# Moving ten DRAM sums of FFN weight blocks to other items of a two-layer encoder kernel

## The chip, the cores and the metric

The kernel runs on one core of a Trainium2 chip. The metric is device time in microseconds: the median of the runs shown. Lower is better. The engines are named as in the profile: PE is TensorE (matmuls), PEld its weight loads, DVE is VectorE, ACT is ScalarE, POOL is GpSimd, SP is SyncE, which here only issues DMAs.

## The reference

Two layers, sequence 512, model width 1024, all in float32. Each layer mixes tokens in three branches of the same input, gates and sums them, projects, normalises, and ends with a SwiGLU feed-forward network:

```python
for l in range(DEPTH):
    h = x @ w_in[l]
    rq, rk, rv, rg, cq, ck, cv, dq, dk, dv, gates = split(h)
    o_a = retention(rq, rk, rv, rg)
    o_b = chunk_attention(cq, ck, cv, ca_rel_bias[l])
    o_c = diff_attention(dq, dk, dv, lam)
    g = sigmoid(gates + b_merge[l])
    merged = g[0]*(o_a @ w_branch_a[l]) + g[1]*(o_b @ w_branch_b[l]) + g[2]*(o_c @ w_branch_c[l])
    x = layer_norm(ALPHA*x + merged @ w_out[l])
    u_gate, u_up = split(x @ w_ffn_in[l])
    x = layer_norm(ALPHA*x + (silu(u_gate)*u_up) @ w_ffn_out[l])
```

The FFN's hidden width is 2816. Retention has 4 heads, the chunk attention 8, the differential attention 4.

## The kernel before, in words

**Arithmetic.** Every float32 operand of a matmul is carried as a pair of rounded parts, high and low; `mm3` (L131 to L134) makes a product of three matmuls. A weight block is loaded into a staging tile `st`; ACT casts it into the high part `wh` (L164 or L385), DVE subtracts to get the low part `wl` (L165 or L392). There are four staging tiles (`NSTAGE`) and three pairs of `wh` and `wl` (`AHEAD`), so loads and casts run up to three blocks ahead of PE.

**Sums of weight blocks.** The large projections use a product of 2x2 blocks with seven block products in place of eight. For that, some products need sums of two or more blocks of the same weight matrix. The sums are made by DMA: POOL issues a DMA whose data is added to what its destination holds (`accum_op=ALU.add`, "an accumulate" below). Mostly that goes into a staging tile (`more`, L191). For the fifth column block of `w_ffn_in` (class `KnownEarly`, two sums) and two row groups of `w_ffn_out` (class `KnownAll`, four sums each) the sums are made long before, in DRAM, by `Known.step` (L325 to L336). Each of these ten steps a layer has two parts: `begin` makes a DRAM tile and has SP copy a first block of 1 MB into it (L331), ordered after the DMA that SP was given last; `end` has POOL add a second block (L335), which waits until the copy has landed. The FFN later loads the finished sums as plain blocks.

The steps in order are in0a, in0c, out00y, out00x, out00c, out00h, out01y, out01x, out01c, out01h (the first digit is the layer, so in1a and so on in the second). out00x adds out00y to its own copy, out00h adds out00x; out01x and out01h likewise.

**The order of the work.** A layer's token mixer is a hand-written list of items in `layer`. An item is a set of weight blocks, a function that issues its matmuls, and groups of smaller steps that `between` calls after each half of it. `run_items` issues them in that order, loads ahead; the framework's scheduler then places each instruction in its engine's queue, so an instruction with few dependencies can stand earlier in a queue than its step stands in the list. Each engine runs its queue in order.

In the list, counted from 0 with the layer's opening items, 18 to 29 are the end of retention (heads 2 and 3, first projections of the second branch, gate of the third), 30, 31, 33 and 35 are the first branch's output (`u_branch(0, i)`) beside the heads of the chunk attention, 36 to 47 the second branch's output and the differential attention, 48 to 54 the third branch, 55 on the output projection `w_out` (`out_items`, whose class `Late` also accumulates on POOL).

In `u_branch` the gate's tile `th` of the first branch comes back from DRAM: SP loads it (L1297), and DVE multiplies it with the branch's product in PSUM, `pt` (L1299). Around it DVE does the softmax of the chunk attention: `tb` is a bias table loaded by SP (L1091), the reduction at L557 reads the scores `psc` and releases their PSUM bank, ACT exponentiates (L559), DVE scales (L1108), PE transposes (`ptr`, L572), ACT and DVE split the result in `cPh` and `cPl` (L116, L122), and PE multiplies them with the values into `pco` (L1142). `memset`s of `kl` on POOL (L514, L515) clear halves of new key tiles.

POOL also computes the power `rsr` of the retention's and the differential attention's norms (L1024, L1234) from a sum `ss` of DVE; DVE scales the head with it (`do`, L1237) and PE transposes it (`pdt`, L1247).

Before the change, one step ends and the next begins at every second item from 30 on:

```python
SUMS_AT = range(30, 52, 2)
...
sums = [list(fns) for fns in zip([lambda: None, *ends], [*begins, lambda: None])]
```

so the begins stand at 30, 32, ... 48 and the ends at 32, 34, ... 50.

Of the kernel before, what the change touches and what calls it, by code (L numbers as in the profile page):

```python
# [51 lines left out]


GROUPS = [(0, 4), (8, 4)]
SUMS_AT = range(30, 52, 2)
REST = 16


# [1 line left out]
def trunk(ctx, tc, x_in, xT_in, w_in, ret_norm_g, da_norm_g, lq1, lk1, lq2, lk2, w_a, w_b, w_c, b_merge, w_out,  # L60
# [614 lines left out]
    def item(specs, fn, *groups):  # L675

        items.append((specs, fn, groups))
# [84 lines left out]
    def layer(l):  # L762
# [80 lines left out]
        def u_rqk(dst, base, hp):  # L843
            def fn(wt):
                for j in range(2):
                    rqk_done(dst, 2 * hp + j, proj_T(xT, wt, P * j))
                    between()
            return [([wcols(base + 256 * hp, 256)], KT)], fn
# [97 lines left out]
        def s_dh(h):  # L946
            def fn():
                dhs[h] = g(name="dh")
                nc.sync.dma_start(dhs[h], decay[h])
            return fn  # L950
# [3 lines left out]
        def s_kt(h):  # L954
            def fn():
                r = rkf.pop(h)
                ps = bank("pkt")
                for mt in range(2):
                    sl = slice(P * mt, P * mt + P)
                    nc.tensor.transpose(ps[:, sl], r[:, sl], ident)  # L960
                kT[h] = HalfPair("kT")
                for mt in range(2):
                    sl = slice(P * mt, P * mt + P)
                    split(kT[h], ps[:, sl], cols=sl, scale=rcol[:, 6 * h + mt:6 * h + mt + 1])
            return fn

        def s_kv(h):
            def fn():
                k, hp, hc = kT.pop(h), h // 2, slice(256 * (h % 2), 256 * (h % 2) + 256)
                ps = bank("pkv")[:, :256]  # L970
                for mt in range(2):
                    sl, vp = slice(P * mt, P * mt + P), rv[hp, mt]
                    mm3(ps, k.hi[:, sl], k.lo[:, sl], vp.hi[:, hc], vp.lo[:, hc], mt == 0, mt == 1)
                kv[h] = HalfPair("kv")
                split(kv[h], ps)
            return fn

        def s_r1(h):
            def fn():
                dh = dhs.pop(h)  # L980
                rp[h] = [Pair("rp"), HalfPair("rp")]
                q, k = rq.pop(h), rk.pop(h)
                rqb[h] = q[1]
                for b, w in enumerate((256, P)):
                    ps, tmp = bank("psr"), g(name="rtmp")
                    for i in range(2):
                        mt = b + 2 * i
                        msl, o = slice(P * mt, P * mt + P), w * i
                        mm3(ps[:, o:o + w], k.hi[:, msl], k.lo[:, msl], q[i].hi[:, P * b:], q[i].lo[:, P * b:], True, True)
                    if b == 0:  # L990
                        nc.vector.tensor_mul(tmp, ps, dh)
                    else:
                        nc.vector.tensor_mul(tmp[:, :P], ps[:, :P], dh[:, :P])
                        nc.vector.scalar_tensor_tensor(tmp[:, P:2 * P], ps[:, P:2 * P], SHIFT[h], dh[:, 2 * P:3 * P],
                                                       op0=ALU.mult, op1=ALU.mult)
                    split(rp[h][b], tmp[:, :2 * w], cols=slice(0, 2 * w))
            return fn
# [39 lines left out]
        def s_r3(h):  # L1037
            def fn():
                os_ = rps.pop(h)
                for d in range(2):  # L1040
                    ps = bank("prt")
                    for nt in range(NT):
                        nc.tensor.transpose(ps[:, P * nt:P * nt + P],
                                            os_[nt // 2][:, 256 * (nt % 2) + P * d:256 * (nt % 2) + P * d + P], ident)
                    oa[2 * h + d] = Pair("oa")
                    split(oa[2 * h + d], ps, scale=v["rg"][:, d:d + 1])
            return fn
# [16 lines left out]
        def v_back(dst):  # L1064
            def fn():
                for k, away in list(dst.items()):
                    dst[k] = g(F32R, "vhl")
                    nc.sync.dma_start(f(dst[k]), away)
            return fn
# [8 lines left out]
        def u_cqk(p):  # L1078
            def fn(wt):
                cqk[p] = QK()  # L1080
                cqk[p].set_q(proj_T(xT, wt, 0), -CA_DH ** -0.5)
                between()
                cqk[p].set_k(proj_T(xT, wt, P))
            return [([wcols(CQ + P * p, P), wcols(CK + P * p, P)], KT)], fn
# [27 lines left out]
        def s_c2(h):  # L1112
            def fn():
                cP[h] = triangle("cP")
                transpose_triangle(cE.pop(h), cP[h])
            return fn
# [155 lines left out]
        def u_gate(br, i):  # L1272
            def fn(wt):
                for j, d in enumerate(tiles(br, i)):
                    gate_done(br, d, proj_T(xT, wt, P * j), (br, i) in EARLY)
                    between()
            return [(cols_of(W, GATE + D * br, br, i), KT)], fn
# [39 lines left out]
        def s_mleft(k):  # L1317
            def fn():
                mq[k].left(acc[k], acc[k + 4], 0.5)
            return fn  # L1320
# [11 lines left out]
        def c_narrow(h):  # L1332
            return lambda: cqk[h // 2].narrow(h % 2)

        def d_narrow(h, j):
            return lambda: dqk[h].narrow(j)

        def c(i):

            return (([s_c3(i - 2, c_narrow(i))] if i >= 2 else []) + [s_c1(i)],  # L1340
                    [s_c2(i - 1)] if 0 <= i - 1 < CA_HEADS else [])

        def d(i):

            h, j = divmod(i, 2)
            if j == 0:
                mid = [s_d4(h - 2)] if h >= 2 else []
                mid += [s_d2(h - 1)] if h >= 1 else []
            else:
                mid = [s_d3(h - 1)] if h >= 1 else []  # L1350
            return mid, [s_d0(h, j)]
# [82 lines left out]
        fifth = KnownEarly(f"in{l}", w_ffn_in[l], 0, 4, (512 * 4, FFN + 512 * 4))  # L1434
        out_blocks = [KnownAll(f"out{l}{i}", w_ffn_out[l], *gr) for i, gr in enumerate(GROUPS)]
        begins, ends = zip(*(st for hv in [fifth] + out_blocks for st in hv.steps()))
        sums = [list(fns) for fns in zip([lambda: None, *ends], [*begins, lambda: None])]
        o = proj = out_items()

        def u_rvg(hp):  # L1440
# [15 lines left out]
        for at, ((specs, fn), *groups) in enumerate(start + [  # L1456
            (w["x"], [p["a"]]), (u_gate(0, 3), [s_kt(0)], [s_kt(1)]), (w["g"],), (w["h"], [p["c"]]),
            (p["m1"], [s_dh(0)]), (p["y"], [], [s_r1(0)]), (p["v"], [s_dh(1)]), (p["m2"], [], [s_r1(1)]),
            (p["x"], [q["a"]]), (u_rqk(rq, RQ, 1), [s_kv(0)], [s_kv(1)]), (p["g"], [q["c"]]), (p["h"],),
            (q["m1"], [], [s_r2(0)]), (q["y"], [s_r2(1)]), (u_rqk(rk, RK, 1), [], [s_r3(0)]),  # L1460
            (q["v"], [s_dh(2)]), (q["m2"], [s_r3(1), s_kt(2)], [s_kt(3), s_r1(2)]), (q["x"], [s_dh(3)]), (u_cqk(0), [], [s_kv(2)]), (q["g"], [s_kv(3)], [s_r1(3)]), (q["h"],),
            (u_gate(2, 0), [s_r2(2)], [s_r2(3), s_r3(2)]), (u_cqk(1), [s_r3(3)] + c(0)[0], c(0)[1]),
            (u_branch(0, 0), c(1)[0] + [v_back(cv)], c(1)[1]), (u_branch(0, 1), *c(2)), (u_cqk(2), *c(3)),
            (u_branch(0, 2), *c(4)), (u_cqk(3), *c(5)), (u_branch(0, 3), *c(6)), 
            (u_dqk(0), [s_c2(6), s_c3(5, c_narrow(7))], [s_c1(7)]), (u_gate(1, 0), [s_c3(6)], [s_c2(7)]),
            (u_dqk(1), [v_back(dv), s_c3(7, d_narrow(0, 0))] + d(0)[1]), (u_branch(1, 0), *d(1)),
            (u_gate(1, 1), [], d(2)[1]), (u_branch(1, 1), [s_d2(0)], d(3)[1]), (u_dqk(2), [s_d3(0)]),
            (u_gate(1, 2), *d(4)), (u_branch(1, 2), *d(5)), (u_dqk(3),),
            (u_gate(1, 3), *d(6)), (u_branch(1, 3), *d(7)), (u_gate(2, 1), [gates_in(2, 0), s_d4(2)], [s_d2(3)]),
            (u_gate(2, 2), [s_d3(3)], [rows_in, s_d4(3)]),  # L1470
            (u_branch(2, 0), [o["a"]], [s_mleft(0)]), (u_branch(2, 1), [], [s_mleft(1)]), (u_gate(2, 3), [s_mright(0)], [s_mright(1), o["c"]]),
            (u_branch(2, 2),), (u_branch(2, 3), [], [s_mleft(2), s_mleft(3)]),
            (o["m1"], [s_mright(2)]), (o["m2"], [s_mright(3)]), (o["y"],), (o["v"],), (o["x"], [norm_rows]),
            (o["g"], [], [s_turned(0)]), (o["h"],),
        ]):
            if at in SUMS_AT:
                groups.append(sums[SUMS_AT.index(at)])
            item(specs, fn, *groups)


        hid = [None] * FT
# [296 lines left out]
```

## Time and profile before

| | |
|---|---|
| median of 3 runs | 1859.38 us (1859.22 to 1859.66) |
| the profiled execution | 1861.9 us, its span 1860.1 us |
| granted clock of TensorE | 0.999 |
| DMA | 344.85 MB, mean 185 GB/s |
| POOL waiting for the copy of in0a, at 287.59 us | 30.43 us |
| POOL waiting for the copy of out01y, at 395.04 us | 16.19 us |

Times are microseconds from the span's start. In a timeline a row is: start, duration, engine, line, operation, output<-inputs, shape, and in brackets the idle time of the engine before it with what ended it. "SPq" is SP's queue. A row of the DMAs gives the tile and its source, the queue that issued it, the count, the size and the median time from issue to landing. A list of waits names who waited for whom, with the total, the number of times and the longest.

### The profile page before, as it was taken

The page shows a single profiled execution, that of the slowest core. Times are in us where ns is not written, and L with a number is a line of the kernel's source. Part 1 is how long each engine was busy: PE and PEld are TensorE (multiplying, and loading weights), DVE is VectorE, ACT ScalarE, POOL GpSimd, SP SyncE. Part 2 cuts the span into 40 slices and gives each one's busy share as a digit, 9 for nine tenths or more (in the row PEclk, how much of TensorE's full clock was granted, in tenths as well). Part 3 has the DMA queues.
Part 4 walks back from the last instruction along what each step waited for, and adds up shares of the span by engine and source line. Part 5 has one row for each costly group of instructions (what it writes and reads, how often), then busy time and mean ns, then how long its engine had stood idle before and what let it go on. Part 6 is the DMA issues. An engine that isn't in the chain of part 4 may idle for free. (4 is left out here: it accounts for less than half of the span.)

```text
span 1860.1 us, 23455 instructions
## 1 busy us (share of the span) xinstructions
PE 1845.1 (99%) x8772; PEld 1539.5 (83%) x8772; DVE 1380.5 (74%) x2102; ACT 1019.6 (55%) x1645; POOL 140.6 (8%) x156
## 2 busy tenths in 40 slices
PE   9999999999999999999999999999999999999998
PEld 7888888788887888888888888888888878888887
DVE  6766755777669786689696777566776797866997
ACT  5555554576645645565465556555766465455551
POOL 2001000011001000000020010001010010000000
PEclk9999999999999999999999999999999999999999
DMA  9685447796475866774586844568955677767652
GB/s 291 177 270 151 124 142 221 186 248 166 133 206 149 197 221 159 184 235 147 182 244 186 245 120 143 169 175 216 254 142 153 176 179 183 210 171 186 225 175 75
DMA packets 244706, 344.85 MB, mean 185 GB/s; under 512 B 9316, under 2 KB 111824, under 8 KB 244592
## 3 DMA queue, kind: packets, MB, share of 16 engines
q1 hardware_dynamic: 213024, 281.84, 45.7%
q0 software_dynamic: 31424, 61.26, 19.1%
q8 instruction: 69, 1.13, 0.2%
q14 instruction: 45, 0.37, 0.1%
q10 hardware_dynamic: 144, 0.26, 0.0%
HBM read 321.25 MB, written 64.01 MB: 207 GB/s over the span
## 5 line engine op out<-in xcount | busy, mean ns | idle before, releaser
L392 DVE TENSOR_TENSOR wl<-st,wh 128x2048 fp32r<-128x2048 f32 (+1 forms) x159 | 353.0, 2222 | 138.2 <-ACT wh L385 131.2
L385 ACT CAST wh<-st 128x2048 fp32r<-128x2048 f32 x154 | 294.1, 1913 | 218.8 <-PE pf L134 110.6
L132 PE MATMUL pt<-xTh,wh 128*128 128x512 f32 x832 | 327.6, 394 | 0.5 <-DVE mx L557 0.5
L133 PE MATMUL pt<-xTl,wh 128*128 128x512 f32 x832 | 324.3, 390 | 0.2 <-DVE xTl L740 0.2
L134 PE MATMUL pt<-xTh,wl 128*128 128x512 f32 x832 | 324.4, 390 | 0.0
L165 DVE TENSOR_TENSOR wl<-st,wh 128x1024 fp32r<-128x1024 f32 (+2 forms) x170 | 177.8, 1064 | 58.6 <-ACT wh L164 54.1
L164 ACT CAST wh<-st 128x1024 fp32r<-128x1024 f32 (+2 forms) x170 | 153.3, 924 | 86.5 <-PE pt L133 53.3
L134 PEld LDWEIGHTS pt<-xTh,wl 128*128 128x128 f32 x832 | 156.3, 188 | 33.2
L132 PEld LDWEIGHTS pt<-xTh,wh 128*128 128x128 f32 x832 | 156.7, 188 | 32.5 <-DVE mx L557 1.2
L133 PEld LDWEIGHTS pt<-xTl,wh 128*128 128x128 f32 x832 | 156.5, 188 | 31.5 <-DVE xTl L740 0.5
L132 PE MATMUL pf<-wh,xTh 128*128 128x512 f32 x384 | 151.0, 394 | 0.2
L134 PE MATMUL pf<-wh,xTl 128*128 128x512 f32 x384 | 149.3, 391 | 0.1
L133 PE MATMUL pf<-wl,xTh 128*128 128x512 f32 x384 | 149.2, 389 | 0.0
L132 PE MATMUL pf<-wh,s12h 128*128 128x512 f32 x288 | 113.7, 395 | 0.0
L132 PE MATMUL pf<-wh,s43h 128*128 128x512 f32 x288 | 112.9, 392 | 0.0
L133 PE MATMUL pf<-wl,s12h 128*128 128x512 f32 x288 | 112.3, 390 | 0.0
L133 PE MATMUL pf<-wl,s43h 128*128 128x512 f32 x288 | 112.2, 390 | 0.0
L134 PE MATMUL pf<-wh,s43l 128*128 128x512 f32 x288 | 111.9, 390 | 0.0
L134 PE MATMUL pf<-wh,s12l 128*128 128x512 f32 x288 | 111.7, 390 | 0.0
L911 ACT COPY tc<-pf 128x512 f32<-128x512 f32 x96 | 54.9, 587 | 76.7 <-PE pf L134 75.9
L132 PEld LDWEIGHTS pf<-wh,xTh 128*128 128x128 f32 x384 | 72.1, 188 | 17.2 <-ACT xTh L116 1.5
L134 PEld LDWEIGHTS pf<-wh,xTl 128*128 128x128 f32 x384 | 72.1, 188 | 16.1 <-DVE xTl L122 0.7
(392 smaller groups left out, 3741.1 us busy)
## 6 DMA issues: line engine op xcount, KB each, us to landing
st<-in_w_in SPq DMA_DIRECT2D x53, 1024.0 KB, 6.6
st<-in_w_ffn_in SPq DMA_DIRECT2D x46, 1024.0 KB, 5.3
st<-in_w_in SPq DMA_DIRECT2D x48, 512.0 KB, 5.2
st<-in_w_ffn_in POOLq DMA_DIRECT2D x20, 1024.0 KB, 11.0
st<-in_w_ffn_out SPq DMA_DIRECT2D x16, 1024.0 KB, 5.1
st<-in_w_in POOLq DMA_DIRECT2D x12, 1024.0 KB, 11.5
th<-th SPq DMA_DIRECT2D x40, 256.0 KB, 6.1
st<-in_w_out SPq DMA_DIRECT2D x10, 1024.0 KB, 5.1
```

The costliest lines, as they stand in the source:

```text
L132: nc.tensor.matmul(ps, lh, rh, start=start, stop=False, skip_group_check=onto)
L133: nc.tensor.matmul(ps, lh, rl, start=False, stop=False, skip_group_check=onto)
L134: nc.tensor.matmul(ps, ll, rh, start=False, stop=stop, skip_group_check=onto)
L164: return [nc.scalar.copy(self.hi[:, a:b], self.st[:, a:b]), nc.vector.tensor_sub(self.lo[:, a:b], self.st[:, a:b], f(self.hi[:, a:b]))]
L165: nc.vector.tensor_sub(self.lo[:, a:b], self.st[:, a:b], f(self.hi[:, a:b]))]
L385: nc.scalar.copy(self.hi, st)
L392: nc.vector.tensor_sub(self.lo[:, k], self.st[:, k], f(self.hi[:, k]))
L911: nc.scalar.copy(t[to, j], ps)
```

## The change

The rule "every second item" is replaced by two tables, one for the ten copies and one for the ten accumulates, and an item may have both. The steps, their order, their sizes and the blocks they read stay the same, and so does everything that reads the sums.

```diff
 GROUPS = [(0, 4), (8, 4)]
-SUMS_AT = range(30, 52, 2)
+COPIED_AT = [18, 21, 24, 27, 37, 40, 43, 45, 47, 49]
+ADDED_AT = [21, 24, 27, 29, 40, 43, 45, 47, 49, 51]
 REST = 16
...
         begins, ends = zip(*(st for hv in [fifth] + out_blocks for st in hv.steps()))
-        sums = [list(fns) for fns in zip([lambda: None, *ends], [*begins, lambda: None])]
+        sums = {}
+        for at, fn in [*zip(ADDED_AT, ends), *zip(COPIED_AT, begins)]:
+            sums.setdefault(at, []).append(fn)
...
-            if at in SUMS_AT:
-                groups.append(sums[SUMS_AT.index(at)])
-            item(specs, fn, *groups)
+            item(specs, fn, *groups, sums.get(at, []))
```

in0a, in0c, out00y and out00x are copied at 18, 21, 24 and 27 and added to at 21, 24, 27 and 29; the other six are copied from 37 to 49 and added to from 40 to 51. No step stands at 30 to 36 any more. The file has one line more than before, so every line from 56 on is one higher in the changed kernel. Instructions that are the same in both kernels can stand in another order in their engine's queue, as the scheduler places them anew; the numbers behind the names of tiles shift with them. Three places:

SP's queue in the first branch of layer 0, around the load of the fifth gate tile (th_2824, source th0_0_4), with bias tables (tb) and the next weights (st); before:

```order
L1091 DMA tb_2727<-nrel_85 128x512
L331 DMA in0c_2814<-in_w_ffn_in 128x4x512
L160 DMA st_3417<-in_w_branch_b 128x4x256
L1297 DMA th_2824<-th0_0_4_583 128x512
L1091 DMA tb_2868<-nrel_85 128x512
L1297 DMA th_2899<-th0_0_5_626 128x512
```

Now:

```order
L1092 DMA tb_2737<-nrel_85 128x512
L161 DMA st_3418<-in_w_branch_b 128x4x256
L332 DMA out00c_3517<-in_w_ffn_out 128x4x512
L1298 DMA th_2831<-th0_0_4_583 128x512
L1092 DMA tb_2875<-nrel_85 128x512
L1298 DMA th_2906<-th0_0_5_626 128x512
```

The copy of in0c ahead of the weights is gone, and the copy of out00c has come up between the weights and the gate tile.

DVE's queue at the same place: the end of one head (cot), the gate's multiply (th, with the product pt), and the softmax's reductions (cE and mx, from the scores psc) of the next head; before:

```order
L1147 TENSOR_TENSOR cot_2852<-pco_2853,cos_2865 64x512
L1299 SCALAR_TENSOR_TENSOR th_2824<-th_2824,pt_2826 128x512
L557 ISA cE_2871,mx_2875<-psc_2876,tb_2727 128x512
L557 ISA mx_2875 128x1
L557 ISA cE_2872,mx_2875<-psc_2881,tb_2727 128x384
```

Now:

```order
L1148 TENSOR_TENSOR cot_2859<-pco_2860,cos_2872 64x512
L558 ISA cE_2878,mx_2882<-psc_2883,tb_2737 128x512
L558 ISA mx_2882 128x1
L558 ISA cE_2879,mx_2882<-psc_2888,tb_2737 128x384
L558 ISA mx_2882 128x1
L558 ISA cE_2880,mx_2882<-psc_2893,tb_2737 128x256
L558 ISA mx_2882 128x1
L1300 SCALAR_TENSOR_TENSOR th_2831<-th_2831,pt_2833 128x512
```

The gate's multiply has moved behind three of the four reductions.

POOL's queue in the second branch's items of layer 0, with two accumulates, the clearing of a key tile (kl) and the first power of a differential head (rsr_4014); before:

```order
L335 DMA out01x_4299<-out01y_4063 128x4x512
L514 MEMSET kl_3939 64x512
L515 MEMSET kl_3940 64x512
L335 DMA out01c_4517<-in_w_ffn_out 128x4x512
L1234 TENSOR_TENSOR rsr_4014<-ss_3981,mhalf_83 128x4
```

Now:

```order
L515 MEMSET kl_3939 64x512
L516 MEMSET kl_3940 64x512
L336 DMA out01x_4353<-out01y_4184 128x4x512
L1235 TENSOR_TENSOR rsr_4014<-ss_3981,mhalf_83 128x4
L336 DMA out01c_4630<-in_w_ffn_out 128x4x512
```

The power now stands ahead of the accumulate of out01c, not behind it.

## The prediction

> **What bounds the kernel now.** I read the page first, then PE's waits, then the stages by windows, then the timelines where PE waits.
>
> ```profile
> span 1860.1 us, 23455 instructions
> PE 1845.1 (99%) x8772; PEld 1539.5 (83%) x8772; DVE 1380.5 (74%) x2102; ACT 1019.6 (55%) x1645; POOL 140.6 (8%) x156
> ```
>
> PE is busy for 1845.1 of 1860.1 us. A change that adds and drops no matmul can win only what PE waits, and the list of waits (total us, times, longest) is short:
>
> ```profile
> PE pco L1142 <- DVE cPl L122: 3.2, 6, 1.1
> ...
> PE ptr L572 <- DVE th L1299: 0.8, 1, 0.8
> PE pdt L1247 <- DVE do L1237: 0.8, 2, 0.5
> PE pt L132 <- DVE mx L557: 0.5, 3, 0.2
> ```
>
> That is 5.3 us in 12 waits, all for DVE. The windows (stretch, length, busy us of PE, PEld, DVE, ACT, POOL) tell where:
>
> ```profile
> 260.00:302.00 42.00, 42.00 (x213) 35.61 (x212) 27.83 (x67) 22.88 (x48) 2.36 (x3) 1.00 0.68 206
> 302.00:364.00 62.00, 59.99 (x307) 49.84 (x306) 39.88 (x94) 34.46 (x73) 5.82 (x7) 1.00 0.68 176
> ...
> 1230.00:1290.00 60.00, 57.42 (x295) 47.95 (x295) 38.79 (x94) 32.84 (x70) 5.82 (x7) 1.00 0.66 172
> ```
>
> The first branch of layer 0 lacks 2.01 us of PE, that of layer 1 2.58 us; from 260 to 302 nothing is lacking. Why is DVE late there? Its timeline, and its own row in the list of waits:
>
> ```profile
> 322.62 0.69 DVE L1299 SCALAR_TENSOR_TENSOR th<-th,pt 128x512 f32<-128x512 f32 x1 [5.20 <-DMA th<-th]
> ...
> 331.20 0.69 DVE L122 TENSOR_TENSOR cPl<-ptr,cPh 128x512 fp32r<-128x512 f32 x1
> ```
>
> ```profile
> DVE th L1299 <- DMA th<-th: 21.4, 4, 6.2
> ```
>
> Four times, two per layer, DVE stands about 5 us before the gate's multiply (L1299 in u_branch), because the gate tile th has not landed. DVE works in order: the next head's softmax and the low parts cPl stand behind it. PE meets that in its longest wait:
>
> ```profile
> 330.67 0.22 PE L533 MATMUL psc<-kl,qs 128*128 128x128 f32 x1
> 331.94 0.39 PE L1142 MATMUL pco<-cPl,vhl 128*64 128x384 f32 x1 [1.05 <-DVE cPl L122]
> 332.17 0.22 PE L1142 MATMUL pco<-cPh,vhl 128*128 128x128 f32 x1
> 332.23 0.22 PE L1142 MATMUL pco<-cPl,vhl 128*64 128x128 f32 x1
> ```
>
> From start to start it is 1.27 us after a 128x128 matmul, where 0.06 is usual: 1.21 us lost, 0.16 more than the 1.05 shown as idle, since the recorded length of a matmul outlasts its turn. For 12 such waits, 5.3 us shown make 5.3 + 12 x 0.16 = 7.2 us lost.
>
> [...]
>
> **Why th is late.** The DMAs issued from 310 to 318, and one th that moved at 250 with nothing beside it (count, KB each, us to landing):
>
> ```profile
> in0c<-in_w_ffn_in POOLq DMA_DIRECT2D x1, 1024.0 KB, 10.5
> st<-in_w_branch_b SPq DMA_DIRECT2D x1, 512.0 KB, 9.2
> th<-th SPq DMA_DIRECT2D x2, 256.0 KB, 7.1
> ```
>
> ```profile
> th<-th SPq DMA_DIRECT2D x1, 256.0 KB, 2.0
> ```
>
> ```profile
> 310.48 1.25 POOL L335 DMA_DIRECT2D in0c<-in_w_ffn_in  x1 [15.49 <-DMA in0c<-in_w_ffn_in]
> ```
>
> The accumulate of in0c (a DRAM sum's second half), issued at 310.48, lands at 321.0, so it is under way when th is loaded: 7.1 us instead of 2.0.
>
> **The change part by part: first branch.** SP's queue around the first of layer 0's two waits (shown with the change above) has lost the copy of in0c, and its accumulate is gone too; but the copy of out00c, whose step stands at 37, is issued right ahead of th. Its price comes from the same pair further on (DMAs issued from 386 to 389) and SP's times:
>
> ```profile
> out01y<-in_w_ffn_out SPq DMA_DIRECT2D x1, 1024.0 KB, 6.7
> st<-in_w_branch_b SPq DMA_DIRECT2D x1, 512.0 KB, 3.6
> ```
>
> ```profile
> 312.71 0.38 SPq L160 DMA_DIRECT2D st<-in_w_branch_b  x1
> ...
> 315.06 0.34 SPq L1297 DMA_DIRECT2D th<-th  x1
> ```
>
> Issued at about 313.1, the copy lands at 319.8 and th some 0.7 behind it, at 320.5; in the trace th came when DVE went on, at 322.6. That is 2.1 us sooner, and the accumulate of out00c begins only afterwards. DVE's own order has moved as well at this place. Three of the softmax's four reductions no longer stand behind th. So cPl comes at least 2.1 us sooner, and PE misses it by 1.2. At the second wait of each layer neither a copy nor an accumulate is left ahead of th. I take the waits of pco, ptr and pt as gone: 3.2 + 0.8 + 0.5 = 4.5 us shown in 10 waits, with the hidden part 4.5 + 1.6 = 6.1 us; bounds 0 and 6.1.
>
> **Third branch.** GpSimd (POOL) issues accumulates and computes the norm's power rsr in one order. DVE's sum ss that rsr needs, and what POOL did:
>
> ```profile
> 437.46 0.16 DVE L1233 SCALAR_TENSOR_TENSOR ss<-ss,sums 128x4 f32<-128x4 f32 x1 [1.01 <-ACT junk L1229]
> 440.01 1.26 POOL L335 DMA_DIRECT2D out01c<-in_w_ffn_out  x1 [13.10 <-DVE wl L165]
> 440.77 1.56 POOL L1234 TENSOR_TENSOR rsr<-ss,mhalf 128x4 f32<-128x4 f32 x1
> ```
>
> rsr could start at 437.6 and starts at 440.8, behind an accumulate that waits for its copy. That is PE's wait pdt. In the changed queue out01c now follows rsr. The wait goes: 0.8 + 2 x 0.16 = 1.1 us; bounds 0 and 1.1. The next rsr comes 20 us later, behind out01c, whose copy needs some 7.
>
> **Retention's end.** in0a and in0c come between the retention heads' weights, and on POOL around rsr:
>
> ```profile
> 164.91 2.00 ACT L164 CAST wh<-st 128x1024 fp32r<-128x1024 f32 x2
> ...
> 174.31 3.02 POOL L1024 TENSOR_TENSOR rsr<-ss,mhalf 128x4 f32<-128x4 f32 x1 [25.48 <-DVE ss L1023]
> 179.42 1.02 POOL L1024 TENSOR_TENSOR rsr<-ss,mhalf 128x4 f32<-128x4 f32 x1 [2.09 <-DVE ss L1023]
> ...
> 180.86 0.39 PE L132 MATMUL pt<-xTh,wh 128*128 128x512 f32 x1
> ```
>
> A load under an accumulate is 9.2 - 3.6 = 5.6 us late (branch_b above). The weights that ACT casts at 164.91 are used at 180.86: 16 us cover it. in0c's accumulate now stands between the two rsr and waits for its copy; should that come after 179, the second rsr would wait, and behind it DVE with that head's scaling and all later casts. The copy is begun three items ahead and takes some 7 us, so I expect no such wait. I cost this part at 0; without the cover each of four accumulates a layer costs up to 5.6 us. [...]
>
> **End of the third branch.** out01h's copy moves behind the eight residual loads z, its accumulate behind the last rsr. z on SP, the accumulates on POOL, what reads w_out's first block, and how long w_out's accumulate takes (DMAs issued from 520 to 545):
>
> ```profile
> 509.85 4.48 SPq L579 DMA_DIRECT2D z<-in_x  x8
> ...
> 510.07 1.27 POOL L335 DMA_DIRECT2D out01h<-out01x  x1 [13.76 <-DMA out01h<-in_w_ffn_out]
> 529.55 1.34 POOL L191 DMA_DIRECT2D st<-in_w_out  x1 [11.83 <-DVE th L1299]
> ...
> 542.63 1.90 ACT L385 CAST wh<-st 128x2048 fp32r<-128x2048 f32 x1
> ...
> 544.56 2.29 DVE L392 TENSOR_TENSOR wl<-st,wh 128x2048 fp32r<-128x2048 f32 x1 [0.43 <-ACT wh L385]
> ```
>
> ```profile
> st<-in_w_out POOLq DMA_DIRECT2D x1, 1024.0 KB, 8.5
> ```
>
> Issued at 514.3, the copy lands near 521 and the accumulate near 532 (6.7 and 10.5 us as above). w_out's own accumulate starts about 3 us later than 529.55 and lands at 541. The branch weights above landed at 312.7 + 9.2 = 321.9, 0.9 us behind the accumulate beside them; w_out's first block, twice their size, comes 1.6 to 3 us behind, at 542.6 to 544. The cast of 542.63 is then up to 1.5 us late, and behind it DVE, which has 0.43 us of room, up to 1.1. Bounds 0 and 1.1 us a layer; I take the middle, 0.5, twice 1.0.
>
> **Sum.** -6.1 - 1.1 + 1.0 = -6.2 us. The profiled execution took 1861.9 us, its span 1860.1 of them, and would take 1855.7. The median of the three runs is 1859.38, 2.5 below that execution; the same 6.2 us give 1853.2.
>
> **The rivals.** *The first branch keeps its first waits*: out00c's copy and accumulate do there what in0c's did. For it: the queue above. Against: th gains 2.1 us, and three reductions pass it. If it holds, about half of the 6.1 stays: 1859.4 - 3.1 = 1856.3.
>
> *The accumulates are not the cause*: th is late by its own queue (weights and tb ahead of it), and only the third branch gains: 1859.4 - 1.1 + 1.0 = 1859.3. Against: 2.0 against 7.1 us.
>
> *Slower, by the end of the third branch*: w_out's first block waits out a whole accumulate more, 8.5 us, and DVE, after its 0.43 us of room, hands 8.1 us per layer on to PE. The gains are 7.2 us in all, so from 3.6 us a layer on nothing is won, and from 5.5 on the kernel is slower by more than 3.7. At 8.1 it is 16.2 - 7.2 = 9.0: 1868.4. For it: two accumulates in a row ahead of that block. Against: from 510.07 to 529.55 lie 19 us, in which the first has room.
>
> **How the numbers follow.** A measurement of this kernel tells about 0.2% (3.7 us) from no change. Forecast 0.70, all faster. First rival 0.15, within 0.2%; second 0.08, within 0.2%; slower rival 0.07. So faster 0.70, same 0.23, slower 0.07. Range: low is the full 7.2 us without the cost, 1852.2, and 1.2 more as my allowance for waits of PE too short for its list, 1851.0; high is the first rival with the full cost of 2.2 in place of 1.0, 1857.5, moved on to 1858.8 to take in half of the second.
>
> **What would show it.** DVE's wait at the gate's multiply: from 21.4 us to under 8. PE's waits for cPl and th: under 1.5 us in all; pdt's row gone. The windows 302:364 and 1230:1290 with under 1 us of PE idle. No PE wait from 140 to 260. PE idle near 560 to 600 grown by no more than 2 us. I am wrong if the waits on th go and the time does not follow, or if PE waits appear at w_out or at rsr of the retention.

## The result, and the profile after

| | before | after |
|---|---|---|
| median of 5 runs each | 1859.38 us (1857.77 to 1861.83) | 1851.11 us (1850.62 to 1851.85) |
| ratio, 95% interval | | 0.9955 (0.994 to 0.9969) |
| profiled execution, its span | 1861.9, 1860.1 us | 1851.1, 1849.3 us |

The change makes the kernel 8.3 us faster (0.45%); 6.2 us were forecast. The two profiled executions lie 10.8 us apart, since that of before was 2.5 us above its median. The page after:

```profile
span 1849.3 us, 23461 instructions
PE 1840.1 (99%) x8772; PEld 1539.2 (83%) x8772; DVE 1380.5 (75%) x2102; ACT 1021.5 (55%) x1645; POOL 140.8 (8%) x156
```

PE does the same 8772 matmuls with 5.0 us less "busy" time. That is no faster matmul: a matmul's recorded length outlasts its turn (at 329.02 below, 0.22 us are recorded and the next starts after 0.06), so the first part of a wait counts as busy (the prediction's hidden 0.16 us). The list of PE's waits and the row of the gate's multiply in DVE's:

```profile
PE warm L716 <- POOL ident masks.py:199: 1.5, 1, 1.5
```

```profile
DVE th L1300 <- DMA th<-th: 6.0, 4, 2.4
```

The waits for cPl, th, pdt and mx are gone; the one left stands at the kernel's start, and stood there before. DVE's own wait fell from 21.4 to 6.0 us. The stretches of the first branch, and two around the first rsr of the differential attention (430 to 460 and 1350 to 1385), after:

```profile
302.00:364.00 62.00, 62.00 (x321) 52.59 (x320) 43.40 (x101) 36.24 (x77) 3.38 (x5) 1.00 0.53 145
430.00:460.00 30.00, 30.00 (x155) 25.64 (x154) 22.20 (x51) 22.12 (x57) 4.45 (x5) 1.00 0.66 149
1230.00:1290.00 60.00, 60.00 (x309) 50.94 (x308) 42.75 (x97) 35.19 (x76) 4.63 (x6) 1.00 0.58 157
```

and of before, the two that were not shown:

```profile
430.00:460.00 30.00, 29.57 (x153) 24.85 (x153) 19.60 (x39) 20.40 (x51) 2.33 (x2) 1.00 0.71 174
...
1350.00:1385.00 35.00, 34.44 (x179) 29.03 (x179) 24.35 (x56) 23.48 (x60) 4.01 (x5) 1.00 0.71 166
```

The second number is PE's busy time: no idle time is left where 2.01, 0.43, 2.58 and 0.56 us were. DVE at the first wait of layer 0, and the matmul of PE that waited 1.05 us before (pco from cPl, 128x384), with the one in front of it:

```profile
318.08 0.08 DVE L558 DVE_READ_ACCUMULATOR2_ANT mx<- 128x1 f32 x1
320.52 0.69 DVE L1300 SCALAR_TENSOR_TENSOR th<-th,pt 128x512 f32<-128x512 f32 x1 [2.36 <-DMA th<-th]
...
326.85 0.68 DVE L123 TENSOR_TENSOR cPl<-ptr,cPh 128x512 fp32r<-128x512 f32 x1
```

```profile
329.02 0.22 PE L534 MATMUL psc<-kl,qs 128*128 128x128 f32 x1
329.08 0.34 PE L1143 MATMUL pco<-cPl,vhl 128*64 128x384 f32 x1
```

DVE still waits for th, 2.4 us in place of 5.2, but with three reductions already done. cPl is finished at 327.5, some 1.5 us before PE comes to it, and the matmul follows the one in front by 0.06 us, where it was 1.27.

POOL's accumulate in the first branch, and what it does at the first rsr of the differential attention now:

```profile
320.38 1.30 POOL L336 DMA_DIRECT2D out00c<-in_w_ffn_out  x1 [26.07 <-DMA tb<-nrel]
...
433.47 1.03 POOL L1235 TENSOR_TENSOR rsr<-ss,mhalf 128x4 f32<-128x4 f32 x1 [7.80 <-DVE ss L1234]
448.52 1.32 POOL L336 DMA_DIRECT2D out01c<-in_w_ffn_out  x1 [14.02 <-DMA out01c<-in_w_ffn_out]
453.72 1.03 POOL L1235 TENSOR_TENSOR rsr<-ss,mhalf 128x4 f32<-128x4 f32 x1 [3.88 <-DVE ss L1234]
```

out00c's accumulate starts when th has all but landed. Both powers wait for nothing but their sum ss.

**Where the time came from.** For each matmul I took the distance from its start to the next one's start, less the usual distance of its kind, and added up what is over. The total is 29.9 us before and 19.0 after, so all of the 10.8 us is there (to the rounding). By place: the first branch (320 to 400 and 1240 to 1320) 8.2 before, 0.9 after; the start of the differential attention (400 to 480 and 1320 to 1400) 6.0 and 3.6; w_out (520 to 640 and 1440 to 1560) unchanged; the kernel's first 80 us 3.4 and 2.8, which the change does not touch. So 7.3 us come from the first branch, 2.3 to 2.4 from the start of the differential attention (the prediction's third branch), 0.7 from the kernel's start, and the rest, some 0.5, is scattered. The times of the same matmul in both traces say it too: those of before are 0.7 us late at 40 and still at 320, 4.3 at 400, 5.4 at 480, 5.8 at 1240, 9.7 at 1320 and 10.9 at 1400.

### The profile page after: what moved, and what is told of

It is laid out like the page before. It is cut to its first block, busy times and chain, and to the rows that moved or that the text cites. A ratio compares the mean times of both kernels' runs of the same rounds, so it can differ in the third digit from the quotient of the medians.

```text
span 1849.3 us, 23461 instructions
## 1 busy us (share of the span) xinstructions
PE 1840.1 (99%) x8772; PEld 1539.2 (83%) x8772; DVE 1380.5 (75%) x2102; ACT 1021.5 (55%) x1645; POOL 140.8 (8%) x156
```

## The experiments

The theory: an accumulate beside the load of th, or ahead of rsr on POOL, makes a short operation late, and what stands behind it on its engine with it. Rivals: DVE's changed order is what counts; or the copies; or the last six steps. Ratios are to the kernel before, run beside each.

**1. Only the first four steps moved.**

```diff
-COPIED_AT = [18, 21, 24, 27, 37, 40, 43, 45, 47, 49]
-ADDED_AT = [21, 24, 27, 29, 40, 43, 45, 47, 49, 51]
+COPIED_AT = [18, 21, 24, 27, 38, 40, 42, 44, 46, 48]
+ADDED_AT = [21, 24, 27, 29, 40, 42, 44, 46, 48, 50]
```

> Only the first four steps (in0a, in0c, out00y, out00x) are moved to the end of retention, the last six are copied and added where the kernel before has them. Theory (the accumulates in the first branch made its gate tile late, and the loss there is made of that): all of the first branch's gain, 6 to 7.3 us, and nothing of the third branch's, as the power rsr stands behind out01c again: 1852 to 1853.5 us, PE's waits for cPl and th gone, the row of pdt there with about 0.8 us. Rival 1 (the gain in the first branch came from DVE's changed order around the gate's multiply, which at the first of the two waits is here as before): under half of it, 1855.5 us or more. Rival 2 (the last six steps bring most of the gain): 1857 us or more.

1853.80 us (1852.11 to 1854.67), ratio 0.9967 (0.9955 to 0.998): 5.6 us gained, 0.3 outside the expected span of times. The rows of the waits that are left, of PE and of DVE for th:

```profile
PE pdt L1248 <- DVE do L1238: 1.9, 2, 1.5
```

```profile
DVE th L1300 <- DMA th<-th: 2.5, 5, 0.7
```

The first branch has no wait of PE left (62.00 of 62.00 us busy), although the multiply stands ahead of the four reductions there, as before: with th this early (DVE waits 0.2 us for it at the first place, until 316.8), DVE's order does not matter. But the wait at pdt is larger than before the change, 1.9 us in place of 0.8. PE's last matmul ahead of it now starts 4.5 us sooner (437.5 for 442.0), but out01c's accumulate, which rsr stands behind, only 3.3:

```profile
436.69 1.26 POOL L336 DMA_DIRECT2D out01c<-in_w_ffn_out  x1 [13.22 <-DMA out01c<-in_w_ffn_out]
437.46 1.56 POOL L1235 TENSOR_TENSOR rsr<-ss,mhalf 128x4 f32<-128x4 f32 x1
```

A wait that a first cure leaves alone can grow by it.

**2. Only the last six steps moved.**

```diff
-COPIED_AT = [18, 21, 24, 27, 37, 40, 43, 45, 47, 49]
-ADDED_AT = [21, 24, 27, 29, 40, 43, 45, 47, 49, 51]
+COPIED_AT = [30, 32, 34, 36, 37, 40, 43, 45, 47, 49]
+ADDED_AT = [32, 34, 36, 38, 40, 43, 45, 47, 49, 51]
```

> The reverse: the first four steps stay in the first branch, the last six are copied and added as in the changed kernel. Theory: the first branch keeps its waits, DVE stands before the gate's multiply for 4 to 6 us each time, and only the third branch gains 1.1 to 2.3 us: 1857 to 1858.5 us. Rival 1 (DVE's order; three of the softmax's four reductions stand ahead of the multiply at the first wait here too): another 2 to 3 us gained in the first branch though the gate tile is as late as before: 1854 to 1855.5 us. Rival 2 (the last six steps bring most of the gain): 1853 us or less.

1857.99 us (1856.48 to 1860.89, 11 runs), ratio 0.9993 (0.9984 to 1.0002): 1.5 us by the medians, as the theory had it, though the interval reaches past 1. PE's waits for cPl and DVE's for th:

```profile
PE pco L1143 <- DVE cPl L123: 3.5, 6, 1.1
```

```profile
DVE th L1300 <- DMA th<-th: 22.1, 5, 5.7
```

th is as late as before, and PE waits for cPl as before. Three reductions ahead of the multiply shorten the way from it to the last cPl (6.3 us in place of 8.6), but th lands at 323.4, 2.9 us later than in the changed kernel, as in0c's accumulate runs beside it and out00c's copy stands ahead of it as well. The windows 302 to 364 and 1230 to 1290 still lack 1.7 and 2.3 us of PE, where the kernel before lacks 2.0 and 2.6. 5.6 and 1.5 make 7.1 of the 8.3 us; the missing 1.2 is about what the wait at pdt grew by in experiment 1 (1.9 - 0.8 = 1.1).

**3. No accumulates.** The kernel before with `end` emptied. It leaves out the ten second blocks, so the FFN reads unsummed copies of the same size.

```diff
-                more = self.sums[second] if isinstance(second, str) else self.src(*second)
-                nc.gpsimd.dma_start(self.sums[key], more, accum_op=ALU.add)
+                pass
```

> The kernel before without the ten accumulates: the copies stay where they are, the second blocks are not added, so that the FFN reads unsummed copies of the same size. Theory (the accumulates slow the loads, the copies hardly): the gate tile lands in about 3 us instead of 7, PE's waits for cPl, th and pdt are gone, 1850.5 to 1852 us. Rival (the copies in SP's queue ahead of the gate tile make it late): DVE still waits 3 us or more each time before the gate's multiply, 1855 us or more.

1851.06 us (1850.55 to 1851.45), ratio 0.9954 (0.9942 to 0.9967). DMAs issued from 310 to 318:

```profile
st<-in_w_branch_b SPq DMA_DIRECT2D x1, 512.0 KB, 3.5
th<-th SPq DMA_DIRECT2D x2, 256.0 KB, 3.0
```

th lands in 3.0 us in place of 7.1, with all ten copies still made where they were. So in the kernel before the accumulates make it late. This does not clear copies in general: here in0c's copy was through before th was issued (from 310 to 313 no DMA moved anything), so none ran beside it. A copy right ahead of th does hold it up, as the changed kernel shows below (5.7 us to landing). And the kernel without these accumulates is no faster than the changed kernel (1851.11) that does all of them: nothing that they cost is left to win.

**4. The same accumulates, another order on DVE.** In the first branch, the softmax step is written ahead of the gate's multiply; the sums stay where they were.

```diff
                     ps = proj_T(act, wt, P * j, nk=nk)
+                    if br == 0:
+                        between()
                     nc.vector.scalar_tensor_tensor(t, t, 1.0, ps, op0=ALU.add, op1=ALU.mult)
...
-                    between()
+                    if br:
+                        between()
```

> The kernel before with all ten steps at their places; in the first branch the softmax step that stood behind the gate's multiply in the program is written ahead of it. Theory (the late gate tile costs PE something only because the softmax's reductions stand behind the multiply on DVE): the gate tile is as late as before, DVE has other work meanwhile, and most of the first branch's loss goes, 4 to 6 us: 1853 to 1855.5 us, the row of pdt still there. Rival (the tile is late for PE too, whose product waits in PSUM for the multiply, whatever DVE's order): the waits go over to the product's PSUM banks and the time stays within 1.5 us of before, 1858 us or more.

1853.21 us (1852.71 to 1854.18), ratio 0.9966 (0.9954 to 0.9979): 6.2 us gained with every accumulate in its old place. DVE at the first wait, and th among the DMAs issued from 310 to 318:

```profile
318.17 0.28 DVE L557 CUSTOM_DVE_ANT_0 cE<-psc,tb 128x128 f32<-128x128 f32 x1
318.38 0.07 DVE L557 DVE_READ_ACCUMULATOR2_ANT mx<- 128x1 f32 x1
321.42 0.69 DVE L1301 SCALAR_TENSOR_TENSOR th<-th,pt 128x512 f32<-128x512 f32 x1 [2.96 <-DMA th<-th]
...
326.96 0.68 DVE L122 TENSOR_TENSOR cPl<-ptr,cPh 128x512 fp32r<-128x512 f32 x1
```

```profile
th<-th SPq DMA_DIRECT2D x2, 256.0 KB, 6.5
```

th takes 6.5 us here, but all four reductions pass it, and the last cPl comes 5.5 us behind the start of the multiply, where it came 8.6 behind before (331.20 and 322.62). PE's waits in the first branch are gone, that at pdt is left. So PE felt next to nothing of the late tile itself; it felt the queue behind it. Either cure is enough alone, if it goes all the way: a tile that is there in time (experiment 1), or an order in which none of the four reductions stands behind it (this one).

**5. One accumulate put back beside th**, run twice, five and seven times:

```diff
-COPIED_AT = [18, 21, 24, 27, 37, 40, 43, 45, 47, 49]
-ADDED_AT = [21, 24, 27, 29, 40, 43, 45, 47, 49, 51]
+COPIED_AT = [18, 32, 24, 27, 37, 40, 43, 45, 47, 49]
+ADDED_AT = [21, 34, 27, 29, 40, 43, 45, 47, 49, 51]
```

> The changed kernel with one step put back: in0c is copied and added again in the first branch, ahead of the first gate tile; DVE's order stays the changed kernel's. Theory (one accumulate beside the gate tile's load is enough to make it late, three reductions now ahead of the multiply hide a part): DVE waits 4 us or more at the first multiply of each layer, PE loses 1 to 2 us a layer there, 1853 to 1855 us. Rival (the changed order on DVE hides all of it): 1850.5 to 1851.8 us, no wait of PE for cPl.

> The kernel with in0c put back in the first branch once more, since its five times lay between 1850.65 and 1856.95 us and its profiled execution was the longest of them. Theory (how late the gate tile lands against the reductions that now stand ahead of its multiply differs from one execution to the next): times spread over 3 us or more again, the median 0.5 to 2 us above the changed kernel's 1851.1, and a profiled execution of under 1852 us shows DVE's wait at the multiply but PE short of it. Rival (the one long time was chance of another kind): all within 1850.5 to 1852.3 us.

1851.94 us (1850.65 to 1856.95) and 1853.80 us (1851.79 to 1858.37), ratios 0.996 (0.9947 to 0.9972) and 0.997 (0.9959 to 0.998). The first median lies 0.1 us above the range that the rival had at first, the second inside the theory's of 1853 to 1855, though 2.7 us above the changed kernel where the second expectation said 0.5 to 2. The single executions spread over 6 to 7 us, where the changed kernel's spread over 1.2. The longest wait of the first profiled execution is in layer 1 (the second has one of 6.6 us there):

```profile
1245.88 0.69 DVE L1300 SCALAR_TENSOR_TENSOR th<-th,pt 128x512 f32<-128x512 f32 x1 [6.47 <-DMA th<-th]
...
1252.21 0.68 DVE L123 TENSOR_TENSOR cPl<-ptr,cPh 128x512 fp32r<-128x512 f32 x1
```

So one accumulate, with out00c's copy ahead of th as in the changed kernel, is enough to make th late again. In layer 0 the new order on DVE hides a part of it: th lands at 323.1, no sooner than before, and the window 302 to 364 lacks 0.8 us of PE in place of 2.0. In layer 1, where th lands 10.2 us after its issue, the window 1230 to 1290 lacks 2.2 in place of 2.6. Both profiled executions were the longest of their runs. That a short one would show th late and PE short of it, as expected for the second try, was not seen and stays open. Why th is later in one execution than in the next, I did not find out.

**6. All ten sums in a row.** They stand from item 9 to 29, so they begin ahead of the place where the changed kernel has four.

```diff
+COPIED_AT = [9, 11, 13, 15, 17, 18, 21, 23, 25, 27]
+ADDED_AT = [11, 13, 15, 17, 19, 21, 23, 25, 27, 29]
```

> All ten sums of a layer are made at the end of retention, so that their accumulates follow each other there. Theory (where the loads have 16 us of room, an accumulate beside them costs nothing; the first, second and third branch have none beside them): no wait of PE for th, cPl or pdt, 1850.5 to 1852 us. Rival (the room is for one accumulate at a time; a row of them starves the weights of the retention heads, or the powers rsr there stand behind them on POOL): PE waits for wh, wl or the retention's transposes of 2 us or more a layer, 1855 us or more.

1897.18 us (1894.02 to 1898.08), ratio 1.0195 (1.0181 to 1.0209): 37 us slower than before. The theory as I put it is wrong here, the rival right. DMAs issued from 154 to 164, and PE's waits:

```profile
st<-in_w_in SPq DMA_DIRECT2D x2, 1024.0 KB, 28.9
...
out00x<-out00y POOLq DMA_DIRECT2D x1, 1024.0 KB, 13.8
```

```profile
PE pt L133 <- DVE ro L1031: 18.7, 2, 10.6
PE pf L133 <- DVE tc L927: 11.3, 2, 6.6
PE prt L1044 <- DVE oal L125: 3.6, 1, 3.6
```

A weight block takes 28.9 us, far past the 16 us that covered one load at the end of retention. ACT's casts wait 10.0 and 5.6 us for two such blocks, while a power rsr stands 1 us behind an accumulate; so of the rival's two ways it is mainly the weights. Room of this kind is a budget, and ten sums overdraw it. How much of it there is at items 9 to 17 was not measured, so how many of the ten would still be free stays open.

**7. One step moved by one item.** The kernel before, with out01c copied at 47 and added at 49:

```diff
+COPIED_AT = [30, 32, 34, 36, 38, 40, 42, 44, 47, 48]
+ADDED_AT = [32, 34, 36, 38, 40, 42, 44, 46, 49, 50]
```

> The kernel before with one step moved by one item: out01c is copied at 47 and added at 49, so that the first power rsr of the differential attention stands ahead of its accumulate on POOL; the first branch is as before. Theory (rsr behind an accumulate that waits for its copy is the whole loss of the third branch): the waits pdt and the one for a score's bank behind it go, 1.1 to 2.3 us: 1857 to 1858.5 us. Rival (late loads in the third branch): rsr is on time, but PE still waits there, 1859 us or more.

1856.75 us (1854.77 to 1859.39, 11 runs), ratio 0.9985 (0.9977 to 0.9994): 3.1 us by medians, which the spread makes uncertain to about 1.6 either way. Its own stretch, 430 to 460:

```profile
430.00:460.00 30.00, 30.00 (x161) 25.81 (x161) 20.59 (x43) 21.82 (x53) 4.29 (x5) 1.00 0.64 154
```

and from start to start the two places (400 to 480 and 1320 to 1400) lose 3.6 us, the changed kernel's value, and not 6.0. So rsr's place behind out01c, which waits for its copy, is all that was lost there.

**8. out01h later still**, among the loads of w_out:

```diff
-COPIED_AT = [18, 21, 24, 27, 37, 40, 43, 45, 47, 49]
-ADDED_AT = [21, 24, 27, 29, 40, 43, 45, 47, 49, 51]
+COPIED_AT = [18, 21, 24, 27, 37, 40, 43, 45, 47, 52]
+ADDED_AT = [21, 24, 27, 29, 40, 43, 45, 47, 49, 54]
```

> The changed kernel with out01h later still: copied at 52, behind the first load of w_out, and added at 54, behind the first accumulate of w_out. Theory (the end of the third branch cost nothing because w_out's first summed block still lands 1.7 us ahead of its cast; this cover is gone when the copy and its accumulate stand among the loads of w_out): casts of w_out 1 to 4 us late, 0.5 to 3 us a layer, 1852 to 1857 us. Rival (blocks loaded ahead cover this too): 1850.5 to 1851.7 us.

1863.25 us (1861.67 to 1864.80, 11 runs), ratio 1.0016 (1.0007 to 1.0024): 12.1 us above the changed kernel, more than either view had. The accumulates of w_out and of out01h now both run beside the load of w_out issued at 528.3. That load and the cast that needs it, then the stretches around PE's wait (the eighth number is the granted clock):

```profile
st<-in_w_out SPq DMA_DIRECT2D x1, 1024.0 KB, 13.7
```

```profile
542.11 1.91 ACT L386 CAST wh<-st 128x2048 fp32r<-128x2048 f32 x1 [4.96 <-DMA st<-in_w_out]
```

```profile
548.00:554.86 6.86, 2.94 (x13) 1.72 (x11) 6.86 (x11) 3.26 (x4) 0.00 (x0) 0.93 0.52 183
554.86:560.50 5.64, 5.64 (x13) 4.47 (x14) 5.64 (x6) 0.70 (x2) 0.00 (x0) 0.50 0.38 147
```

The cast is late by 4.85 us against the changed kernel's (537.26), and PE waits 3.9 us. Then comes a second price: for 5.6 us TensorE's granted clock is 0.50, and 13 matmuls take the time of some 25. From start to start the wait costs 4.1 us in each layer, which alone is above the expected 0.5 to 3; the half clock, which my expectation left out, adds most of the rest, to 7.3 us in layer 0 and 5.9 in layer 1.

**9. Three kernels with the step set too early.** These were to try experiment 4's order on the changed kernel, on experiment 5's, and on experiment 7's. In all three the call was set one statement too early, ahead of the branch's product and not only of the multiply:

```diff
+                    if br == 0:
+                        between()
                     ps = proj_T(act, wt, P * j, nk=nk)
                     nc.vector.scalar_tensor_tensor(t, t, 1.0, ps, op0=ALU.add, op1=ALU.mult)
```

So their expectations speak of another program:

> The changed kernel, and the softmax step of the first branch written ahead of the gate's multiply as well. Theory (nothing of the first branch's loss is left in the changed kernel, so a second cure of it is worth nothing): 1850.5 to 1851.8 us. Rival (the 2.4 us that DVE still waits at the first multiply cost PE something): 1850 us or less.

> in0c put back in the first branch, with the softmax step written ahead of the gate's multiply. Theory (an accumulate beside the gate tile's load costs something only through DVE's order): 1850.5 to 1851.8 us in every execution, spread under 1.5 us. Rival (the accumulate also delays the first branch's weights and bias tables so that PE meets it): times up to 1853 us or more remain.

> The kernel before with no sum moved out of the first branch: only the softmax step is written ahead of the gate's multiply there, and out01c is copied at 47 and added at 49 so that the first rsr stands ahead of it. Theory (the whole gain is of two places where a short operation stood behind one that waits for a DMA): the sum of both, 1859.6 - 6.2 - 2.3 = 1851.1, within 1850.3 and 1852 us. Rival (that four accumulates more at the retention free the first branch's loads is worth something by itself): 1852.5 us or more.

1886.69, 1887.63 and 1887.26 us, ratios 1.0146 (1.0132 to 1.016), 1.0148 (1.0133 to 1.0164) and 1.0148 (1.0134 to 1.0162). PE's waits in the first of them:

```profile
PE pco L1143 <- ACT cPh L117: 22.1, 6, 4.5
```

The branch's product was what PE did while ACT and DVE computed the softmax; without it PE waits for them, six times, up to 4.5 us, and from 315.6 to 322, behind the second of them (4.1 us), the granted clock was 0.51. What can still be read off: with the sums of the changed kernel (the first) and of nearly the kernel before (the third) the time is the same within 0.6 us. Once PE waits there for something that comes later than th, the first branch's part of the change is worth nothing (the third has rsr ahead of out01c already, as the first has). Whether the two orders alone, correctly set, give all of the gain was not tried; by separate runs (6.2 and 3.1 us) they come to about as much.

## Why the prediction was right, and where its terms were off

| step | forecast | in the traces | by experiment |
|---|---|---|---|
| first branch | -6.1 | -7.3 | -6.2 (exp. 4), -5.6 with a larger pdt (exp. 1) |
| third branch | -1.1 | -2.3 | -3.1, uncertain (exp. 7) |
| retention's end | 0 | 0 | 0 for four sums, not for ten (exp. 6) |
| end of the third branch | +1.0 | 0 | 0, near the edge (exp. 5, 8) |
| kernel's start and scattered | | -1.2 | |
| sum | -6.2 | -10.8 (medians: -8.3) | |

The median of 1851.11 us lies 0.1 above the low end of the forecast range, 1851.0. The working alone ended at 1852.2 there; that the time is inside rests on the 1.2 us that were allowed for waits too short for PE's list. In the traces the gain is 4.6 us over the forecast: 1.2 in the first branch, 1.2 in the third, 1.0 at the third branch's end, and 1.2 at the kernel's start and scattered. By medians it is 2.1 over, since the profiled execution of before was 2.5 us above its median; which terms are smaller in the others, the traces do not tell.

**First branch: right.** th was forecast at 320.5 and the multiply started at 320.52; the mechanism held in both its parts, the tile sooner and the reductions past it. What th waited out is the copy ahead of it, as forecast (DMAs issued from 310 to 318, no accumulate beside them):

```profile
out00c<-in_w_ffn_out SPq DMA_DIRECT2D x1, 1024.0 KB, 7.4
...
th<-th SPq DMA_DIRECT2D x2, 256.0 KB, 5.7
```

With neither copy nor accumulate beside it, th takes 3.0 us at this place (experiment 3). The prediction's 2.0 us, "with nothing beside it", is that of a th on its way out to DRAM, so not of a load; 7.1 against 3.0 says the same. In the changed kernel neither part was run alone as it stands there: experiment 1 has th 3.8 us sooner, experiment 4 all four reductions ahead, and experiment 2, with three ahead but th at 323.4, loses. An estimate: before, the last cPl was finished 9.3 us behind the start of the multiply (322.62 and 331.89). From 320.52 that makes 329.8, 0.7 behind the matmul of 329.08. So here the change needed both. The first rival's premise, out00c's copy and accumulate in in0c's stead, is half there: the copy is issued ahead of th and makes DVE wait 2.4 us, but the accumulate starts at 320.4, behind th. The second rival, accumulates not the cause, falls with experiment 3. The size is 1.2 us over the forecast in the profiled pair: the list's 10 waits do not hold all, since a stop of 0.2 us and shorter ones show only from start to start, and the hidden part was 0.24 us, not 0.16, at the three waits for mx.

**Third branch: right in mechanism, the term too small by 1.2 us.** The forecast counted the two waits of the list, 0.8 + 0.32. From start to start each layer lost 0.5 to 0.6 us ahead of the four transposes, 0.3 between them, as each followed its piece of DVE's scaling, and 0.3 at the next product, 8.8 us later. All of it went when rsr went ahead (experiment 7).

**Retention's end: right, the cover used up further than I saw.** POOL and ACT there, after:

```profile
173.62 3.02 POOL L1025 TENSOR_TENSOR rsr<-ss,mhalf 128x4 f32<-128x4 f32 x1 [23.10 <-DVE ss L1024]
177.00 1.31 POOL L336 DMA_DIRECT2D in0c<-in_w_ffn_in  x1 [0.35 <-issue]
178.75 1.04 POOL L1025 TENSOR_TENSOR rsr<-ss,mhalf 128x4 f32<-128x4 f32 x1 [0.45 <-DVE ss L1024]
```

```profile
165.18 2.00 ACT L165 CAST wh<-st 128x1024 fp32r<-128x1024 f32 x2 [0.85 <-DMA st<-in_w_in]
```

in0c's accumulate found its copy landed between the two rsr, as expected, and the second rsr waited for DVE alone. The cast at 165.18 now waits 0.85 us for a block that took 17.3 us beside two accumulates, in0a's and one of w_in that was there before; with that one alone it took 10.8. So it came 6.5 us later, a little over the 5.6 of the forecast, and 16 us of cover took that without a wait of PE. With more accumulates the cover does not hold: beside a row of them a 1 MB load took 28.9 us (experiment 6).

**End of the third branch: forecast +1.0, measured 0, the low end of its bounds.** Set back by the 5.4 us by which the cast now comes sooner, w_out's accumulate started at 531.3, 1.7 us later than before where 3 were forecast, and took 9.6 us in place of 8.5; so it landed at 540.9, where 541 was forecast, by two errors that cancel. The load that the cast waits for is the plain block issued at 528.4 (533.9 before):

```profile
st<-in_w_out SPq DMA_DIRECT2D x1, 1024.0 KB, 8.7
```

```profile
536.67 0.63 ACT L119 ACTIVATE s43h<-sb 128x512 fp32r<-128x512 f32 x1 [0.85 <-DVE sb L426]
537.26 1.91 ACT L386 CAST wh<-st 128x2048 fp32r<-128x2048 f32 x1
```

It landed at 537.2, 0.1 us before ACT came to it; before, 6.8 us of load ended 2.0 us ahead of the cast at 542.63. So it came 1.6 us behind the accumulate, the near end of the forecast's 1.6 to 3: the room shrank from 2.0 to 0.1 us, and nothing was lost. What was off is the choice of the middle, 0.5 a layer, where the bound of 0 held. In the second profiled execution of experiment 5, whose end of the branch is the changed kernel's, the same load took 11.3 us:

```profile
540.88 1.91 ACT L386 CAST wh<-st 128x2048 fp32r<-128x2048 f32 x1 [2.58 <-DMA st<-in_w_out]
```

PE lost 2.0 us there. So the term was real as a risk, and experiment 8 ran into what the slower rival named, a block held up by one accumulate more; the changed kernel stands just short of it.

Of the signs named beforehand, DVE's wait (6.0, under 8), the rows of PE's waits, both windows, the stretch from 140 to 260 and w_out all came as forecast.

## What to carry to other kernels

In these runs an operation that waited for a DMA held up whatever stood behind it on its engine (5.2 us on DVE at the gate's multiply, 3.2 us for rsr on POOL), and that, not the late tile, was what the busiest engine felt (experiment 4: 6.2 us gained with th still taking 6.5 us): ask for each such operation who is behind it, and either bring the data sooner or put the operation later. A transfer moved to a place with room cost nothing until the room was spent (four sums at the end of retention 0 us, ten 37 us), so measure the room there in microseconds and count what has been put into it. Gains at two such places need not add up: a wait left alone can grow when the work ahead of it gets faster (0.8 to 1.9 us in experiment 1), and a later wait can swallow a gain (experiment 9: 1886.69 us with the sums of the changed kernel, 1887.26 with nearly those of before).

## What the runs showed of the hardware

**Half the clock behind a wait.** After PE's waits of 3.9 us (experiment 8), and after 6.6 us in experiment 6, the 128x512 matmuls started 0.43 us apart in place of 0.23, for 5 to 6 us, at a granted clock of 0.50. Experiment 6:

```profile
156.00:164.40 8.40, 1.89 (x9) 1.23 (x7) 4.19 (x5) 4.96 (x4) 2.54 (x2) 0.73 1.07 338
164.40:170.00 5.60, 5.56 (x13) 4.43 (x14) 4.31 (x6) 2.09 (x6) 1.26 (x1) 0.50 1.11 266
170.00:188.00 18.00, 18.00 (x103) 15.79 (x103) 3.74 (x4) 3.60 (x5) 1.25 (x1) 1.00 1.10 239
```

There is a shorter case too: in experiment 5's layer 1, 0.50 was granted for 3 us behind two waits of 1.18 and 1.05 us with 0.7 us of work between them:

```profile
1249.80:1253.00 3.20, 0.97 (x6) 0.49 (x4) 3.20 (x5) 1.35 (x4) 1.04 (x2) 0.94 1.12 204
1253.00:1256.00 3.00, 3.00 (x12) 2.81 (x13) 2.23 (x4) 1.17 (x2) 0.00 (x0) 0.50 1.08 312
```

In its second profiled execution PE waited three times for cPl, 2.8 us in all and up to 1.3, and once 1.83 us at w_out; behind the latter the matmuls started 0.34 us apart once and then 0.24 to 0.25, and the mean granted clock of the execution was 0.999, where the first had 0.998. How long a wait brings the half clock on, these runs do not show.

**The spread went as well.** The kernel before ran between 1857.5 and 1863.0 us in 21 runs; the five that ran beside the changed kernel lie within 4.1 us, the changed kernel's five within 1.2, those without accumulates within 0.9.
